# A hybrid two-layer decoder in split fp32: products with v of two groups moved behind a later group's scores, into one accumulator bank

## The chip, the core and the metric

The kernel runs on one core of a Trainium2 chip. The metric is the device time of one execution in microseconds (us). TensorE (PE) multiplies, VectorE (DVE) and ScalarE (ACT) work on tiles in SBUF and on PSUM, GpSimd (POOL) does a few small steps, and SyncE (SP) issues the DMAs that load weights.

## What is computed

Two layers on 256 positions of width 1024, 16 heads of 64, all in fp32:

```
h = x
for i in range(DEPTH):
    ln1_g, ln1_b, w1, w2, ln2_g, ln2_b = channel[i]
    h = layer_norm(DEEPNORM_ALPHA * h + mixers[i % N_MIXERS](h), ln1_g, ln1_b)
    h = layer_norm(DEEPNORM_ALPHA * h + squared_relu_mlp(h, w1, w2), ln2_g, ln2_b)
```

Layer 0 mixes by stick-breaking attention, where a weight is a sigmoid times a running product of others:

```
    log_keep = jnp.where(past, -jax.nn.softplus(z), 0.0)
    log_keep_between = lax.cumsum(log_keep, axis=3, reverse=True) - log_keep
    w = jnp.where(past, jnp.exp(jax.nn.log_sigmoid(z) + log_keep_between), 0.0)
    return jnp.einsum('bhqk,bhkd->bhqd', w.astype(v.dtype), v)
```

Layer 1 is block-sparse attention, which at 256 positions is one block: causal softmax attention with rotary positions. The MLP of both layers is `jnp.square(jax.nn.relu(x @ w1)) @ w2` with 4096 hidden values.

## The kernel before

Every fp32 operand of a projection is split into a high and a low part, and three products (high by high, high by low, low by high) make one. A weight comes in units of 1 MB: a DMA into one of three raw buffers (`Unit`, L249), two casts to `hi` on ScalarE and two subtractions to `lo` on VectorE (`split`, L205 and L206), into one of five split buffers. Activations stand transposed as `xh`, `xl`.

The heads of a layer go in four groups of four heads, each group in two pairs. The units of a layer's projections come in the order of `SEQ`: A0 to A3 give q and k of a group, V0 and V1 give v of two groups. Per group the chain is: projection (`qkT` in layer 0, `qk` and the transposes `tp` in layer 1), split of q and k (`qkh`, `qkl`), scores `sc` (`scores`, L438), weights (`weights`, L453), their transposes `pt_ps` (L501), a copy `pt` on ScalarE (L512), the products with v `o` (`mix`, L519) and their split `oh`, `ol`. In layer 0 the weights of a pair are two sigmoids on ScalarE (`keep`, `p`, L462), a scan on VectorE (L466), a mask on GpSimd (L470) and a product on VectorE (L473). In layer 1 they are maxima on VectorE (L479), four exponentials on ScalarE (L490) and a division by the sums (L497). Behind the groups come the output projection (`wo`, L614), LayerNorm (`norm`, L351) and the MLP (`up`, `down`).

PSUM has four accumulator banks (`acc`, one bank each: projections) and two double banks (`wk`, two banks each). The scores of a group take both `wk`, one per pair; each transposition of weights takes one, and so do the products with v of a group. A `wk` with scores comes free when ScalarE has read it for the last time.

The order of the instructions is fixed when the program is built. `Plan` (L64) keeps a clock per engine. An operation is given with an engine, a cost, a rank, what it follows (`after`) and which buffers it takes and gives. Projections are written straight into TensorE's order; the operations of a plan go into an engine's order where its clock lets them start, lowest rank first among those that could start within 0.25 us (`best`, L100). The costs are only used for that; on the chip the engines wait for each other by semaphores, each in its own fixed order. The scores are an operation of 1.55 (layer 0) or 1.8 (layer 1), rank 1, that takes both `wk` (L449); the products with v one of 1.36, rank 0.5, that takes one `wk` (L530).

Of the kernel before, what the change touches and what calls it, by code (L numbers as in the profile page):

```python
# [8 lines left out]
F32R = mybir.dt.float32r  # L9
# [5 lines left out]
P = 128  # L15
D = 1024
T = 256
NT = T // P
KT = D // P
HD = 64  # L20
# [11 lines left out]
MARGIN, WINDOW = 0.5, 0.25  # L32
X_LOADS = {0: 1, 1: 1, 2: 2, 4: 2, 6: 2}
WARM = 8

C_ID = 0
C_COS = C_ID + P
# [117 lines left out]
def trunk(ctx: ExitStack, tc: tile.TileContext, x, xt, cst, cstb, w, ln, out):  # L155
    nc = tc.nc
# [21 lines left out]
    def wbank(name):  # L178
        return wk.tile([P, 2, 512], F32, tag="wk", name=name)
# [231 lines left out]
    for l in range(DEPTH):  # L411
# [6 lines left out]
        def attend(g, pr, src, ready, give):  # L418

            box = {}

            def part(s):
                def go():
                    if s not in box:
                        box[s] = buf("qk" + "hl"[s], F32R)[:, :2 * T]  # L430
                    return box[s]
                return go
            qk = split(2 * T, part(0), part(1), src, after=ready, rank=0.9, take=[("t2k", 2, 2)], give=give)
            both[g].append((box, qk))
            if pr == 0:
                return

            def scores():  # L438
                for y, _ in both[g]:
                    sc = y["sc"] = wbank("sc")  # L440
                    for c0, nk, q0 in ((0, T, T - P), (T, P, 0)):
                        for i, (a, b) in enumerate(((0, 0), (0, 1), (1, 0))):
                            for j in range(2):
                                r = slice(j * HD, (j + 1) * HD)
                                mm(sc[:, j, c0:c0 + nk], y[a][r, q0:q0 + P], y[b][r, T:T + nk], c0 == 0 and i == 0, l == 0 and q0 == 0 and i == 2)
                for y, _ in both[g] if l else ():
                    for j in range(2):
                        mm(y["sc"][:, j, P:3 * P], identb, maskb, False, True)
            s = plan.op("pe", 1.8 if l else 1.55, scores, after=[y for _, y in both[g]], rank=1, take=[("wk", 2)], give=[("t2k", 4)])  # L449
            for q in range(2):  # L450
                weights(g, q, both[g][q][0], s)

        def weights(g, pr, box, s):  # L453
            sc = lambda: box["sc"][:, :, 0:3 * P]
            three = lambda y: y[:, :6 * P].rearrange("p (j e) -> p j e", j=2)
            if l == 0:
                def sig(name, scale):
                    def go():
                        y = box[name] = t3k.tile([P, 772], F32, tag="t3k", name=name)
                        if name == "keep":  # L460
                            nc.gpsimd.memset(y[:, 6 * P:6 * P + 1], 1.0)
                        nc.scalar.activation(three(y), sc(), AF.Sigmoid, scale=scale)  # L462
                    return go
                k = act(6 * P, sig("keep", -SCALE), after=[s], rank=0.7, take=[("t3k", 2)])
                b = act(6 * P, sig("p", SCALE), after=[k], rank=0.69, give=[("wk", 1)])
                c = dve(12 * P, lambda: nc.vector.tensor_tensor_scan(  # L466
                    box["keep"][:, 0:6 * P][:, ::-1], box["keep"][:, 0:6 * P][:, ::-1], ind[:, ::-1], 1.0,
                    op0=ALU.mult, op1=ALU.max), after=[k], rank=0.7)
                late = lambda: three(box["p"])[:, :, P:].rearrange("p j (a e) -> p j a e", e=P)
                z = plan.op("pool", 0.9, lambda: nc.gpsimd.affine_select(  # L470
                    out=late(), in_=late(), pattern=[[0, 2], [0, 2], [-1, P]], compare_op=ALU.is_gt, fill=0.0, base=0,
                    channel_multiplier=1), after=[b], rank=0.69)
                p = dve(6 * P, lambda: nc.vector.tensor_tensor(  # L473
                    box["p"][:, :6 * P], box["p"][:, :6 * P], box["keep"][:, 1:6 * P + 1], op=ALU.mult),
                    after=[z, c], rank=0.69, give=[("t3k", 1)])
            else:
                sm = smalla.tile([P, 16], F32, tag="sma", name="sma")
                part_of = [(0, T), (T, 3 * P)]
                mx = [dve(2 * (b - a), lambda t=t, a=a, b=b: nc.vector.tensor_reduce(  # L479
                    sm[:, 2 * t:2 * t + 2], box["sc"][:, :, a:b], axis=AX.X, op=ALU.max), after=[s], rank=0.7)  # L480
                    for t, (a, b) in enumerate(part_of)]
                ng = dve(10, lambda: nc.vector.tensor_scalar(sm[:, 4:8], sm[:, 0:4], -SCALE, None, op0=ALU.mult), after=mx, rank=0.7)
                ex = []
                for t, (a, b) in enumerate(part_of):
                    for j in range(2):
                        def go(t=t, j=j, a=a, b=b):
                            if t == 0 and j == 0:
                                box["p"] = t3k.tile([P, 772], F32, tag="t3k", name="p")
                            i = 2 * t + j
                            nc.scalar.activation(three(box["p"])[:, j, a:b], box["sc"][:, j, a:b], AF.Exp, scale=SCALE,  # L490
                                                 bias=sm[:, 4 + i:5 + i], accum_out=sm[:, 8 + i:9 + i])
                        ex.append(act(b - a + 290, go, after=[ng] + ex, rank=0.7, take=() if ex else [("t3k", 1)],
                                      give=[("wk", 1)] if t == 1 and j == 1 else ()))
                rc = dve(10, lambda: nc.vector.reciprocal(sm[:, 12:16], sm[:, 8:12]), after=ex, rank=0.65)
                for t, (a, b) in enumerate(part_of):
                    for j in range(2):
                        p = dve((b - a) * 0.54 + 55, lambda t=t, j=j, a=a, b=b: nc.vector.tensor_scalar(  # L497
                            three(box["p"])[:, j, a:b], three(box["p"])[:, j, a:b], sm[:, 12 + 2 * t + j:13 + 2 * t + j], None, op0=ALU.mult),
                            after=[rc], rank=0.65)

            def turn():  # L501
                ps = box["pp"] = wbank("pt_ps")
                for j in range(2):
                    pj = three(box["p"])[:, j, :]
                    nc.tensor.transpose(ps[:, j, 0:P], pj[:, T:T + P], ident)
                    nc.tensor.transpose(ps[:, j, P:T], pj[:, 0:P], ident)
                    nc.tensor.transpose(ps[:, j, T:T + P], pj[:, P:T], ident)
            tp = plan.op("pe", 0.66, turn, after=[p], rank=0.6, take=[("wk", 1)], give=[("t3k", 1)])

            def evac():  # L510
                box["pt"] = pts.tile([P, 2, 384], F32, tag="pt", name="pt")
                nc.scalar.copy(box["pt"], box["pp"][:, :, :384])  # L512
            ev = act(6 * P, evac, after=[tp], rank=0.6, take=[("pt", 1)], give=[("wk", 1)])

            pv[g].append((box, ev))
            if pr == 0:
                return

            def mix():  # L519
                if g // 2 not in OT:  # L520
                    OT[g // 2] = (st.tile([P, 4, T], F32R, tag="sh", name="oh"), st.tile([P, 4, T], F32R, tag="sl", name="ol"))
                o = pv[g][0][0]["o"] = wbank("o")
                for q in range(2):
                    for kt in range(2):
                        for j in range(2):
                            hd = 4 * g + 2 * q + j
                            pt = pv[g][q][0]["pt"][:, j, :]
                            nc.tensor.matmul(o[HD * j:HD * j + HD, q, kt * P:T], v[kt][:, hd * HD:(hd + 1) * HD],  # L528
                                             pt[:, 0:T] if kt == 0 else pt[:, T:T + P], start=kt == 0, stop=kt == 1)
            m = plan.op("pe", 1.36, mix, after=[e for _, e in pv[g]] + [vtok[g // 2]], rank=0.5,  # L530
                        take=[("wk", 1)] + ([("st", 1)] if g % 2 == 0 else []), give=[("pt", 2)])
            ps = slice(2 * (g % 2), 2 * (g % 2) + 2)
            mixed[g, 0] = mixed[g, 1] = split(2 * T, lambda: OT[g // 2][0][:, ps, :], lambda: OT[g // 2][1][:, ps, :],
                                              lambda: pv[g][0][0]["o"][:, :, :T], after=[m], rank=0.8, give=[("wk", 1)])

        def qkT(g, us):
            plan.wait(take=[("acc", 2)])
# [297 lines left out]
```

## Time and profile before

| | us |
|---|---|
| median of 3 runs (lowest, highest) | 595.88 (595.02, 596.15) |
| the profiled execution | 596.54 |
| its span, first to last instruction | 594.5 |
| busy: TensorE, VectorE, ScalarE, GpSimd | 584.9, 391.4, 288.4, 32.7 |
| mean granted TensorE clock | 0.996 |

The profile is of one execution; the span is what the trace covers of it. A TensorE that is busy is not at its peak, since matmuls overlap; what counts is the time from the start of one to the start of the next. In a row of the timeline the first number is the start in us from the span's start, the second the time that it took, and brackets at the end tell how long the engine had been idle and what ended that. On VectorE and ScalarE an instruction can start some 0.1 us before the one ahead of it has ended.

### The profile page before, as it was taken

What the parts mean: (1) busy time and instruction counts of PE and PEld (TensorE: products, weight loads), DVE (VectorE), ACT (ScalarE), POOL (GpSimd) and SP (SyncE); (2) the same over time, 40 slices, a digit from 0 to 9 for tenths busy, and PEclk for the clock granted to TensorE, in tenths of its full rate; (3) what the DMA queues carried; (4) which work ended last, traced back from release to release, by engine and by line L of the source; (5) the groups of instructions that cost most, each with busy time, mean ns of one, the idle gap of its engine ahead of it and who ended that gap; (6) DMA issues with size and microseconds to landing.
All of it is one profiled execution on the core that took longest, in us unless ns stands there. A gap on an engine that the chain in (4) does not pass through costs nothing.

```text
span 594.5 us, 8745 instructions
## 1 busy us (share of the span) xinstructions
PE 584.9 (98%) x3636; PEld 507.5 (85%) x3636; DVE 391.4 (66%) x485; ACT 288.4 (49%) x411; POOL 32.7 (5%) x38
## 2 busy tenths in 40 slices
PE   8999999999999999999999999999999999999995
PEld 6899987889899899898888788778898898899884
DVE  5779784878446555555789777768667437447445
ACT  5756574436444543543535754826446435435410
POOL 0102110000000000000032021000000000000000
PEclk9999999999999999999999999999999999999998
DMA  8977333175546346437175523443674364355101
GB/s 290 388 291 281 142 142 142 71 256 194 211 190 252 146 170 268 156 144 282 66 228 210 203 80 136 142 142 119 236 283 160 149 258 180 151 236 207 78 0 71
DMA packets 17895, 109.25 MB, mean 184 GB/s; under 512 B 1984, under 2 KB 2624, under 8 KB 5824
## 3 DMA queue, kind: packets, MB, share of 16 engines
q1 hardware_dynamic: 17856, 108.70, 49.2%
q8 instruction: 28, 0.46, 0.3%
q14 instruction: 11, 0.09, 0.0%
HBM read 107.64 MB, written 1.05 MB: 183 GB/s over the span
## 4 chain that ended last, share of the span: by engine, by line
PE 89%; DMA 4%; DVE 4%; ACT 1%; issue 1%; SPq 0%; POOL 0%; DVEq 0%; ACTq 0%
PE up_ps L191 29%; PE dn_ps L191 29%; PE wo_ps L191 8%; PE qk_ps L191 7%; PE v_ps L191 6%; DMA raw<-in_wqkv 3%; PE qkT_ps L191 2%; PE sc L191 2%; DVE lo L206 2%; PE o L528 2%; DMA raw<-in_first 1%; PE xt L386 1%; DVE keep L466 1%; ACT hi L205 1%; PE tp L574 1%
## 5 line engine op out<-in xcount | busy, mean ns | idle before, releaser
L206 DVE TENSOR_TENSOR lo<-raw,hi 128x1024 fp32r<-128x1024 f32 (+1 forms) x196 | 228.3, 1207 | 57.0 <-ACT hi L205 55.1
L205 ACT CAST hi<-raw 128x1024 fp32r<-128x1024 f32 (+1 forms) x196 | 191.8, 1032 | 70.5 <-issue 42.4
L191 PE MATMUL up_ps<-xh,hi 128*128 128x256 f32 x384 | 106.4, 277 | 0.0
L191 PE MATMUL up_ps<-xl,hi 128*128 128x256 f32 x384 | 106.1, 276 | 0.0
L191 PE MATMUL up_ps<-xh,lo 128*128 128x256 f32 x384 | 106.1, 276 | 0.0
L191 PE MATMUL dn_ps<-hi,hl 128*128 128x512 f32 x252 | 99.3, 394 | 0.0
L191 PE MATMUL dn_ps<-lo,hh 128*128 128x512 f32 x252 | 98.8, 392 | 0.0
L191 PE MATMUL dn_ps<-hi,hh 128*128 128x512 f32 x252 | 98.0, 389 | 0.0
L648 DVE SCALAR_TENSOR_TENSOR r<-up_ps,r 128x512 f32<-128x512 f32 x32 | 22.0, 687 | 77.9 <-ACT r L646 77.9
L191 PEld LDWEIGHTS up_ps<-xl,hi 128*128 128x128 f32 x384 | 72.1, 188 | 0.5
L191 PEld LDWEIGHTS up_ps<-xh,hi 128*128 128x128 f32 x384 | 72.1, 188 | 0.5
L191 PEld LDWEIGHTS up_ps<-xh,lo 128*128 128x128 f32 x384 | 72.1, 188 | 0.0
L646 ACT ACTIVATE r<-up_ps 128x512 f32<-128x512 f32 x32 | 19.1, 596 | 95.3 <-PE up_ps L191 95.3
L191 PEld LDWEIGHTS dn_ps<-lo,hh 128*128 128x128 f32 x252 | 47.3, 188 | 10.4
L191 PEld LDWEIGHTS dn_ps<-hi,hh 128*128 128x128 f32 x252 | 47.3, 188 | 10.0
L191 PEld LDWEIGHTS dn_ps<-hi,hl 128*128 128x128 f32 x252 | 47.4, 188 | 9.4
L191 PE MATMUL qkT_ps<-xh,hi 128*128 128x256 f32 x128 | 36.9, 289 | 0.0
L191 PE MATMUL qkT_ps<-xh,lo 128*128 128x256 f32 x128 | 36.2, 283 | 0.3 <-DVE lo L206 0.2
L191 PE MATMUL qkT_ps<-xl,hi 128*128 128x256 f32 x128 | 35.9, 280 | 0.0
L366 POOL TENSOR_TENSOR sm<-sm,one 128x1 f32<-128x1 f32 x8 | 7.9, 987 | 425.2 <-DVE sm L365 425.2
L205 ACT CAST xh<-xt 128x512 fp32r<-128x512 f32 x12 | 7.0, 586 | 41.1 <-PE xt L386 41.1
L191 PE MATMUL qk_ps<-hi,xh 128*128 128x512 f32 x64 | 26.3, 411 | 0.0
(106 smaller groups left out, 919.8 us busy)
## 6 DMA issues: line engine op xcount, KB each, us to landing
raw<-in_w SPq DMA_DIRECT2D x64, 1024.0 KB, 4.9
raw<-in_wqkv SPq DMA_DIRECT2D x22, 1024.0 KB, 5.1
raw<-in_wo SPq DMA_DIRECT2D x8, 1024.0 KB, 5.1
raw<-in_first SPq DMA_DIRECT2D x8, 256.0 KB, 5.9
gb<-in_l_ln_g SPq DMA_DIRECT2D x4, 512.0 KB, 3.9
gb<-in_l_ln_b SPq DMA_DIRECT2D x4, 512.0 KB, 5.1
h<-in_x SPq DMA_DIRECT2D x2, 512.0 KB, 7.3
h<-in_xt SPq DMA_DIRECT2D x3, 256.0 KB, 6.1
```

Of the source, the lines that this page charges most:

```text
L191: nc.tensor.matmul(ps, sta, mov, start=start, stop=stop)
L205: f = lambda: nc.scalar.copy(hi(), src())
L206: g = lambda: nc.vector.tensor_tensor(lo(), src(), hi().bitcast(F32), op=ALU.subtract)
L366: pw = plan.op("pool", 1.0, lambda: nc.gpsimd.tensor_tensor(rs, ve, nhalf, op=ALU.pow), after=[ep], rank=0)
L386: nc.tensor.transpose(XB[t, n][:, k * P:(k + 1) * P], h[t][:, (4 * n + k) * P:(4 * n + k + 1) * P], ident)
L466: c = dve(12 * P, lambda: nc.vector.tensor_tensor_scan(box["keep"][:, 0:6 * P][:, ::-1], box["keep"][:, 0:6 * P][:, ::-1], ind[:, ::-1], 1 ...
L528: nc.tensor.matmul(o[HD * j:HD * j + HD, q, kt * P:T], v[kt][:, hd * HD:(hd + 1) * HD], pt[:, 0:T] if kt == 0 else pt[:, T:T + P], start=k ...
L574: nc.tensor.transpose(tb[pr][:, c0:c0 + P], QK[g, t]["qk"][:, e * T + pr * P:e * T + pr * P + P], ident)
L646: nc.scalar.activation(box["r", n], ps, AF.Relu)
L648: return dve(512, lambda: nc.vector.scalar_tensor_tensor(box["r", n], ps, 0.0, box["r", n], op0=ALU.max, op1=ALU.mult), after=[a], rank=0. ...
```

## The change

Groups 0 and 1 of a layer lose their own operation for the products with v. In layer 0 the products of group 0 are issued in the operation of group 1's scores, right behind them, and those of group 1 behind group 2's; in layer 1 those of group 0 behind group 2's scores and those of group 1 behind group 3's (`MIX`). The joint operation costs 1.3 more, waits also for the transposed weights of the old group, and takes one `acc` bank besides the two `wk`. These products write one accumulator bank in place of a half-used double bank; groups 2 and 3 stay as they were. The mask on GpSimd is entered with 1.25 for 0.9.

```diff
+MIX = ({1: 0, 2: 1}, {2: 0, 3: 1})
...
-            s = plan.op("pe", 1.8 if l else 1.55, scores, after=[y for _, y in both[g]], rank=1, take=[("wk", 2)], give=[("t2k", 4)])
+            old = MIX[l].get(g)
+            if old is None:
+                s = plan.op("pe", 1.8 if l else 1.55, scores, after=[y for _, y in both[g]], rank=1, take=[("wk", 2)], give=[("t2k", 4)])
+            else:
+                s = plan.op("pe", 3.1 if l else 2.85, lambda: (scores(), mix(old)), after=[y for _, y in both[g]] + [e for _, e in pv[old]] + [vtok[old // 2]],
+                            rank=1, take=[("wk", 2), ("acc", 1)] + ([("st", 1)] if old % 2 == 0 else []), give=[("t2k", 4), ("pt", 2)])
+                mixed_from(old, s, ("acc", 1))
...
-                z = plan.op("pool", 0.9, lambda: nc.gpsimd.affine_select(
+                z = plan.op("pool", 1.25, lambda: nc.gpsimd.affine_select(
...
-            m = plan.op("pe", 1.36, mix, after=[e for _, e in pv[g]] + [vtok[g // 2]], rank=0.5,
-                        take=[("wk", 1)] + ([("st", 1)] if g % 2 == 0 else []), give=[("pt", 2)])
+            if g not in MIX[l].values():
+                bank = "wk" if g > 1 else "acc"
+                m = plan.op("pe", 1.36, lambda: mix(g), after=[e for _, e in pv[g]] + [vtok[g // 2]], rank=0.5,
+                            take=[(bank, 1)] + ([("st", 1)] if g % 2 == 0 else []), give=[("pt", 2)])
+                mixed_from(g, m, (bank, 1))
+
+        def mix(g):
...
+            o = wbank("o")[:, 0, :] if g > 1 else abank("o")
+            o = pv[g][0][0]["o"] = o.rearrange("p (q t) -> p q t", q=2)
...
+        def mixed_from(g, m, give):
...
-                                              lambda: pv[g][0][0]["o"][:, :, :T], after=[m], rank=0.8, give=[("wk", 1)])
+                                              lambda: pv[g][0][0]["o"], after=[m], rank=0.8, give=[give])
```

The planner then sets every engine's order anew, which the diff doesn't show. Three places follow. A line number of the change stands 2 to 15 above that of the same statement before.

VectorE in layer 0, around group 1's weights (lo8 to lo10 are splits of weight units, qkl those of group 1's q and k, keep the scans, p the products of L473, ol the split of group 0's products with v). Before:

```order
L206 TENSOR_TENSOR lo6_436<-raw6_371,hi6_435 128x1024 x2
L206 TENSOR_TENSOR ol_442<-o_443,oh_441 128x512
L206 TENSOR_TENSOR lo7_486<-raw7_452,hi7_485 128x1024 x2
L206 TENSOR_TENSOR lo8_518<-raw8_473,hi8_517 128x1024 x2
L206 TENSOR_TENSOR qkl_563<-qkT_ps_421,qkh_561 128x512
L206 TENSOR_TENSOR qkl_581<-qkT_ps_422,qkh_570 128x512
L206 TENSOR_TENSOR lo9_579<-raw9_508,hi9_578 128x1024 x2
L206 TENSOR_TENSOR lo10_626<-raw10_544,hi10_625 128x1024 x2
L466 SCALAR_TENSOR_TENSOR keep_640<-keep_640,const_112 128x768
L473 TENSOR_TENSOR p_653<-p_653,keep_640 128x768
L466 SCALAR_TENSOR_TENSOR keep_663<-keep_663,const_112 128x768
L473 TENSOR_TENSOR p_674<-p_674,keep_663 128x768
```

With the change:

```order
L208 TENSOR_TENSOR lo7_485<-raw7_444,hi7_484 128x1024 x2
L208 TENSOR_TENSOR lo8_517<-raw8_473,hi8_516 128x1024 x2
L208 TENSOR_TENSOR qkl_560<-qkT_ps_421,qkh_548 128x512
L208 TENSOR_TENSOR qkl_571<-qkT_ps_422,qkh_555 128x512
L208 TENSOR_TENSOR lo9_566<-raw9_504,hi9_565 128x1024 x2
L208 TENSOR_TENSOR lo10_628<-raw10_543,hi10_627 128x1024 x2
L474 SCALAR_TENSOR_TENSOR keep_636<-keep_636,const_112 128x768
L474 SCALAR_TENSOR_TENSOR keep_659<-keep_659,const_112 128x768
L481 TENSOR_TENSOR p_647<-p_647,keep_636 128x768
L481 TENSOR_TENSOR p_669<-p_669,keep_659 128x768
L208 TENSOR_TENSOR ol_616<-o_617,oh_615 128x512
```

The ol of group 0 went from ahead of lo7 to behind both products, and the second scan now stands ahead of the first product.

ScalarE in layer 1, around group 3's exponentials (p from sc; hi62 and hi63 are casts of wo's units, v1 the copy of v, oh the casts of the products with v). Before:

```order
L205 CAST hi62_3551<-raw62_3342 128x1024 x2
L490 ACTIVATE p_3569,sma_3420<-sc_3521,sma_3420 128x256 x2
L490 ACTIVATE p_3569,sma_3420<-sc_3521,sma_3420 128x128 x2
L490 ACTIVATE p_3588,sma_3421<-sc_3534,sma_3421 128x256
L601 COPY v1_96<-v_ps_3512 128x512
L205 CAST hi63_3593<-raw63_3407 128x1024 x2
L490 ACTIVATE p_3588,sma_3421<-sc_3534,sma_3421 128x256
L490 ACTIVATE p_3588,sma_3421<-sc_3534,sma_3421 128x128 x2
L205 CAST oh_3605<-o_3607 128x512
```

With the change:

```order
L207 CAST hi62_3518<-raw62_3315 128x1024 x2
L207 CAST oh_3384<-o_3563 128x512
L616 COPY v1_96<-v_ps_3473 128x512
L207 CAST hi63_3584<-raw63_3346 128x1024 x2
L498 ACTIVATE p_3590,sma_3405<-sc_3533,sma_3405 128x256 x2
L498 ACTIVATE p_3590,sma_3405<-sc_3533,sma_3405 128x128 x2
L498 ACTIVATE p_3598,sma_3406<-sc_3546,sma_3406 128x256 x2
L498 ACTIVATE p_3598,sma_3406<-sc_3546,sma_3406 128x128 x2
L207 CAST oh_3611<-o_3613 128x512
```

Group 1's oh, the copy of v and the two casts of hi63 now stand ahead of all eight exponentials.

TensorE in layer 1, from group 3's scores to group 2's products with v. Before, eighteen products of v stand between the masks and wo; the last three of them and what follows:

```order
L191 MATMUL v_ps<-hi_3268,xh 128x512
L191 MATMUL v_ps<-lo_3269,xh 128x512
L191 MATMUL v_ps<-hi_3268,xl 128x512
L191 MATMUL wo_ps<-hi_3306,oh 128x512
L191 MATMUL wo_ps<-lo_3307,oh 128x512
L191 MATMUL wo_ps<-hi_3306,ol 128x512
L528 MATMUL o<-pt,v_95 64x256 x2
L528 MATMUL o<-pt,v_96 64x128 x2
```

With the change, from the last mask on:

```order
L193 MATMUL sc<-masks 128x256
L543 MATMUL o<-pt,v_95 64x256 x2
L543 MATMUL o<-pt,v_96 64x128 x2
L543 MATMUL o<-pt,v_95 64x256 x2
L543 MATMUL o<-pt,v_96 64x128 x2
L193 MATMUL v_ps<-hi_3248,xh 128x512
L193 MATMUL v_ps<-lo_3249,xh 128x512
L193 MATMUL v_ps<-hi_3248,xl 128x512
L193 MATMUL wo_ps<-hi_3284,oh 128x512
L193 MATMUL wo_ps<-lo_3285,oh 128x512
L193 MATMUL wo_ps<-hi_3284,ol 128x512
L543 MATMUL o<-pt,v_95 64x256 x2
```

Group 1's products with v follow the masks, fifteen of the eighteen products of v have gone ahead of the scores, and group 2's products with v come after three of v and three of wo.

## Rows read from the trace of the kernel before

**Rows 1.** The page, busy time of each engine.
```profile
PE 584.9 (98%) x3636; PEld 507.5 (85%) x3636; DVE 391.4 (66%) x485; ACT 288.4 (49%) x411; POOL 32.7 (5%) x38
```

**Rows 2.** Waits of TensorE: for whom, us in total, times, longest.
```profile
PE pt_ps L505 <- DVE p L473: 0.5, 1, 0.5
```

**Rows 3.** Layer 0's MLP: stretch, length, busy us (count) by engine, granted clock, DMA.
```profile
131.00:290.00 159.00, 159.00 (x996) 142.42 (x995) 89.92 (x96) 71.28 (x87) 0.99 (x1) 1.00 0.51 194
```

**Rows 4.** TensorE's timeline, layer 0, group 0's products with v.
```profile
33.93 0.28 PE L191 MATMUL qkT_ps<-xh,lo 128*128 128x256 f32 x1
34.13 1.52 PE L528 MATMUL o<-pt,v 128*64 128x256 f32 x16
35.59 0.39 PE L191 MATMUL qkT_ps<-xh,hi 128*128 128x256 f32 x1
35.81 0.28 PE L191 MATMUL qkT_ps<-xl,hi 128*128 128x256 f32 x1
```

**Rows 5.** TensorE's timeline, layer 0, group 1's scores and what follows.
```profile
48.15 0.38 PE L191 MATMUL sc<-qkh 64*128 64x256 f32 x2
48.37 0.28 PE L191 MATMUL sc<-qkl,qkh 64*128 64x256 f32 x2
...
49.67 0.39 PE L191 MATMUL qkT_ps<-xh,hi 128*128 128x256 f32 x1
```

**Rows 6.** ScalarE's and VectorE's timeline, layer 0, group 1's weights.
```profile
43.88 2.00 ACT L205 CAST hi<-raw 128x1024 fp32r<-128x1024 f32 x2 [1.84 <-DMA raw<-in_wqkv]
...
47.24 1.28 DVE L206 TENSOR_TENSOR qkl<-qkT_ps,qkh 128x512 fp32r<-128x512 f32 x2
...
52.98 2.19 DVE L466 TENSOR_TENSOR_SCAN keep<-keep,const 128x768 f32<-128x768 f32 x1
55.27 1.14 DVE L473 TENSOR_TENSOR p<-p,keep 128x768 f32<-128x768 f32 x1
56.33 1.74 DVE L466 TENSOR_TENSOR_SCAN keep<-keep,const 128x768 f32<-128x768 f32 x1
58.18 0.96 DVE L473 TENSOR_TENSOR p<-p,keep 128x768 f32<-128x768 f32 x1
```

**Rows 7.** TensorE's timeline, layer 0, first transpose of group 1's weights.
```profile
56.55 0.30 PE L505 MATMUL pt_ps<-const,p 128*128 128x128 f32 x1 [0.48 <-DVE p L473]
```

**Rows 8.** TensorE's timeline, layer 1, around group 2's products with v.
```profile
381.15 0.39 PE L191 MATMUL v_ps<-hi,xl 128*128 128x512 f32 x1
...
382.17 1.52 PE L528 MATMUL o<-pt,v 128*64 128x256 f32 x16
383.62 0.51 PE L191 MATMUL wo_ps<-hi,oh 128*128 128x512 f32 x1
...
384.20 0.39 PE L191 MATMUL wo_ps<-hi,ol 128*128 128x512 f32 x1
384.43 0.39 PE L191 MATMUL wo_ps<-hi,oh 128*128 128x512 f32 x1
```

**Rows 9.** ScalarE's timeline, layer 1, exponentials of group 3, first and fourth sum.
```profile
378.55 0.47 ACT L490 ACTIVATE p<-sc,sma 128x256 f32<-128x256 f32 x1 [1.07 <-DVE sma L482]
...
380.06 0.21 ACT L490 ACTIVATION_READ_ACCUMULATOR p<-sc,sma 128x1 f32 x1
...
381.58 0.59 ACT L601 COPY v<-v_ps 128x512 f32<-128x512 f32 x1 [0.86 <-PE v_ps L191]
382.06 2.00 ACT L205 CAST hi<-raw 128x1024 fp32r<-128x1024 f32 x2
```

**Rows 10.** TensorE's first products, then stretches behind the last matmul (columns as above).
```profile
1.38 3.60 PE L285 MATMUL warm_ps<-masks 128*128 128x512 bf16 x8 [1.38 <-POOL keep L461]
...
6.26 0.28 PE L191 MATMUL qkT_ps<-xh,lo 128*128 128x256 f32 x1
...
587.10:589.80 2.70, 0.00 (x0) 0.00 (x0) 2.56 (x7) 0.00 (x0) 0.99 (x1) 1.00 0.00 0
589.80:594.50 4.70, 0.00 (x0) 0.00 (x0) 1.45 (x3) 0.00 (x0) 0.00 (x0) 0.51 0.31 112
```

More of the change, by code (lines that the diff above doesn't have):

```diff
@@ L517, in weights @@
                 return
[L519 to L529, printed above, removed]
@@ new lines, in mix @@
+        def mix(g):
+            if g // 2 not in OT:
+                OT[g // 2] = (st.tile([P, 4, T], F32R, tag="sh", name="oh"), st.tile([P, 4, T], F32R, tag="sl", name="ol"))
+            o = wbank("o")[:, 0, :] if g > 1 else abank("o")
+            o = pv[g][0][0]["o"] = o.rearrange("p (q t) -> p q t", q=2)
+            for q in range(2):
+                for kt in range(2):
+                    for j in range(2):
+                        hd = 4 * g + 2 * q + j
+                        pt = pv[g][q][0]["pt"][:, j, :]
+                        nc.tensor.matmul(o[HD * j:HD * j + HD, q, kt * P:T], v[kt][:, hd * HD:(hd + 1) * HD],
+                                         pt[:, 0:T] if kt == 0 else pt[:, T:T + P], start=kt == 0, stop=kt == 1)
```

## Prediction

> **What bounds the kernel now.** I read the page's busy times first: TensorE is busy for 584.9 of 594.5 us [rows 1]. The list of TensorE's waits comes next. After the first microseconds its one entry of note is 0.5 us, a transpose of group 1's weights in layer 0 that waits for VectorE's product at L473 [rows 2]. The table by stretch shows the same for the MLP: TensorE busy for all of 159 us, VectorE for 90 and ScalarE for 71 [rows 3]. So the order of TensorE's work is nearly free of holes, and the end is set by its sum. Two things can change the time: what it loses when it switches between kinds of matmul, and holes that the new order opens. A hole in the attention of either layer is not paid back later, since the MLP behind it runs without any slack on TensorE.
>
> **What a switch costs.** Products of 256 columns start every 0.12 us. The last one before group 0's products with v starts 0.20 us ahead of them, and the first one behind them holds the engine for 0.22 us [rows 4]. So entering costs 0.08, and the first full product after leaving 0.10. The sixteen parts themselves take 1.46 us. The scores take 1.52 from their start to the next projection [rows 5].
>
> In layer 0 the change takes away one entry and one leaving per pair (scores, products with v) and adds one passage from scores to products that no row shows. Bounds of a pair's gain: nothing, if that passage costs as much as both, and 0.36, if it is free (0.08 + 0.10, and as much again for the last parts, which run out before the next kind starts). I take 0.2, near the middle, since the nearest row, the plain passage [rows 4], costs half of that sum; no row shows a passage dearer than an entry and a leaving together, so I leave out a loss. In layer 1 the scores end with mask products over the whole array, so only a passage of the plain kind goes: 0 to 0.2 a pair, taken as 0.1. Two pairs in each layer: **-0.6 us**, between 0 and -1.1. The Trainium skill, in TensorEngine Tiling (Array Packing), Key Properties, says that changing the tiling mode drains the engine; scores are tiles of 64 rows and products tiles of 64 columns, so by it the passage is not free, and -0.6 would shrink to about -0.3.
>
> **Layer 0, group 1's scores.** Without the products of group 0 ahead of them these scores come earlier: 48.15 [rows 5], less 35.59 - 33.93 = 1.66, plus 0.12 for the plain step, less 0.10 for the slow first product [rows 4], plus 0.35 for three products that now stand ahead of them: 46.86. Their third part needs qkl. VectorE makes it from 47.24 on (1.28 for the two, so the first ends at about 47.9) [rows 6], and it can't be earlier: it stands behind two lo of weight unit 8, which wait for two casts that ScalarE began at 43.88, when that unit's load had landed [rows 6]. The change leaves that order as it was but for one ol fewer. The third part was due 0.22 after the start [rows 5], at 47.08, and can run at 48.0: a new wait of **0.9 us**. It lies between 0, should the load land a microsecond earlier, and 1.0. Behind it TensorE has nothing it could do out of order.
>
> **Layer 0, group 1's transposes.** The scores end at 48.0 - 0.22 + 1.52 = 49.3. Products with v follow until 50.7, then 57 projection products of 0.12 with their first slow one: TensorE reaches the transposes at 57.4. They need the first product of L473. Before, VectorE ran scan, product, scan, product: 52.98 for 2.19, 55.27 for 1.14, 56.33 for 1.74, 58.18 for 0.96 [rows 6]. The start of the first scan stays, since four lo stand ahead of it whose loads don't move. Now both scans come first. The second one ends at 55.1 + 1.74 to 2.19 (the two lengths that rows 6 show), the product takes 0.96 to 1.14 behind it, and the transposes follow 0.14 later, as now (55.27 + 1.14 to 56.55 [rows 6, 7]): 58.0 to 58.6. I take 58.35, so a wait of **0.95 us**, bounds 0.6 to 1.2, in the place of the present one of 0.5 [rows 2, 7], **-0.5**. These two waits are tied: if the first is short, TensorE stands the longer at the second, for it is VectorE that sets 58.35. The second product ends 0.9 after the first, and TensorE comes to its transposes 0.95 after it came to the others, so nothing is added there.
>
> The ol of group 0 now comes behind both products on VectorE, at about 59 to 59.7, and until then its accumulator bank is held. Two more banks are next asked for by group 3's projection, some 2 us after that; this costs nothing while that cover stands. The pool operation's new number (1.25 for 0.9) is a due time in the planner and adds no work. Loads keep their sequence on SP.
>
> **Layer 1, group 2's products: the largest term.** Let S be the end of group 3's scores on TensorE. There TensorE used to have eighteen products of v and three of wo in hand before group 2's products with v. Now there are group 1's products with v (1.45), three of v (383.62 to 384.43, as those of wo behind products with v do now: 0.81) and three of wo with the passage (381.15 to 382.17 less one product: 0.79) [rows 8]. TensorE comes to group 2's products at S + 3.05.
>
> These still take a double bank, and both double banks hold group 3's scores until ScalarE has done the exponentials. On ScalarE four things now stand ahead of the first exponential: the cast oh of group 1, the copy of v, and two casts of the last wo unit. The copy can begin 0.43 after the last v product starts (381.15 to 381.58 [rows 8, 9]), and that start is S + 1.45 + 0.58 (383.62 to 384.20), so at S + 2.46; oh is through by then. The copy takes 0.48 (381.58 to 382.06), two casts 2.0, and the first four exponentials with their sums 1.72 (378.55 to 380.06 + 0.21) [rows 9]. The first double bank comes free at S + 6.66. The wait is 6.66 - 3.05 = **3.6 us**; I take 3.5, as the two casts overlap what follows by 0.1, and bounds of 3.2 and 3.8. Behind the waiting products stand the transposes of group 3 and the rest of wo, with nothing else that TensorE could do. VectorE's maxima for that bank, which the exponentials need, stand no later in its order than before and don't decide. Behind the hole all inputs are early, so no further wait follows.
>
> **The clock.** After the last matmul, which ended at 587.1, the granted clock stayed at 1.00 up to 589.8 and was 0.51 after it [rows 10]. So it fell within 2.7 us of idling. TensorE will idle for some 3.4 us in the hole of layer 1 (3.5 less what the last wo product still runs). The nearest row thus says that the clock falls to 1.2 GHz in the hole or just behind it. The price: nothing, if it holds; at most 2.4 us, as at the start, where the eight warm-up products of 512 columns took 0.45 each, twice the usual 0.23 (384.20 to 384.43 [rows 8]), and full speed came at 6.2, 4.8 us after the first of them at 1.38 [rows 10], half of which is lost. I take **1.4 us**, a little above the middle, since by the row the fall comes shortly before work resumes. The Trainium skill, in TensorE: Matmul & The Clock Gate (HAM oscillation), says that a long wait between matmuls throttles the engine again and the next work starts cold; by it the sum keeps this term, without it it would be 1.4 less.
>
> **Sum.** -0.6 + 0.9 + 0.95 - 0.5 + 3.5 + 1.4 = +5.65. The profiled execution took 596.54, 0.66 above the median of the runs, 595.88. On its own time the sum gives 602.2, on the median **601.5 us**. A change within 0.2%, 1.2 us, can't be told from none.
>
> **The rivals.**
> 1. *The clock holds.* Nothing in the trace of before has a hole as long as this in mid-program, so only the end speaks for a fall, and there TensorE never resumes. Time 595.88 + 4.25 = 600.1. By the Trainium skill's rule above this would not happen. Chance 0.36.
> 2. *The lost time is given back, and it comes out not slower.* Place: the MLP. If weights (load, cast, lo) paced TensorE there, the hole of layer 1 would let units run ahead and be recovered. It decides once TensorE shows waits in the MLP. Against it: busy for 159 of 159 us there [rows 3], and only five split units fit. Time 595.88 - 0.6 = 595.3. Chance 0.06.
> 3. *The loads of layer 0 land earlier than in this one execution,* so that both waits there shrink to 0.6 together, and the clock holds: 595.88 - 0.6 - 0.5 + 0.6 + 3.5 = 598.9. Chance 0.05.
> 4. *The change doesn't do what it says:* products of a group could stand apart from the scores. The order of the instructions shows them together at all four places, so I give this no chance of its own.
>
> **How the numbers follow.** Forecast 0.50, the three rivals 0.36, 0.06 and 0.05; 0.03 is left for more than 603.4, should the clock stay low for longer than at the start. The bounds of layer 0's two waits together (0.6 to 2.2), of layer 1's (3.2 to 3.8), of the switches (0 to -1.1) and of the clock (0 to 2.4), with the -0.5, reach from 598.1 to 603.8; I cut this to 599.2 to 603.0, which leaves out rivals 2 and 3 and the ends. Faster by over 0.2%: 0.04, most of rival 2; within 0.2%: 0.04; slower: 0.92.
>
> **What would show it.** Right: a wait of 3 to 4 us by o on ScalarE's p at L498 in layer 1; a wait of near 1 us by sc on qkl and one of near 1 us by pt_ps on L481 in layer 0; a stretch of some 3 us behind the long wait with a granted clock near 0.5 and products of 512 columns at 0.43. Wrong: no such wait of o, or the wait and an unchanged time, or a clock of 1.00 throughout with 600.

## The result, and the profile after

The changed kernel took **599.57 us** (median of 4 runs, 598.70 to 599.96), the kernel before 596.01 (595.02 to 596.16) on the same chip: ratio 1.0062, 95% interval 1.0050 to 1.0074, so it is slower. In a later comparison with more runs of the kernel before it took 600.12 against 595.45, ratio 1.0072 (1.0060 to 1.0085).

| | before | after |
|---|---|---|
| profiled execution, us | 596.54 | 599.2 |
| its span | 594.5 | 597.2 |
| mean granted TensorE clock | 0.996 | 0.995 |

The busy line of the page after, which answers to [rows 1]:

```profile
PE 583.6 (98%) x3636; PEld 507.0 (85%) x3636; DVE 393.5 (66%) x485; ACT 288.3 (48%) x411; POOL 34.4 (6%) x38
```

TensorE has the same number of instructions and is busy for 1.3 us less, in a span that is 2.7 longer. The list of TensorE's waits after, which answers to [rows 2], says where the difference stands (columns: line, tile waited for, us in total, times, longest):

```profile
PE o L543 <- ACT p L498: 3.5, 1, 3.5
PE warm_ps L287 <- POOL keep L469: 1.4, 1, 1.4
PE qkT_ps L193 <- DVE lo L208: 0.7, 3, 0.2
PE qkT_ps L193 <- ACT hi L207: 0.6, 1, 0.6
```

One long wait, the forecast one: group 2's products with v wait for ScalarE's exponentials, 3.5 us. Two forecast waits of layer 0 are not there, neither `sc` on `qkl` nor `pt_ps` on the product of L481. TensorE's timeline of layer 1 after, from group 1's products with v on, answers to [rows 8]:

```profile
376.98 1.52 PE L543 MATMUL o<-pt,v 128*64 128x256 f32 x16
378.43 0.51 PE L193 MATMUL v_ps<-hi,xh 128*128 128x512 f32 x1
...
379.71 0.40 PE L193 MATMUL wo_ps<-hi,ol 128*128 128x512 f32 x1
383.59 2.83 PE L543 MATMUL o<-pt,v 128*64 128x256 f32 x16 [3.48 <-ACT p L498]
386.35 0.51 PE L193 MATMUL wo_ps<-hi,oh 128*128 128x512 f32 x1
```

ScalarE's timeline over the same stretch answers to [rows 9]:

```profile
378.55 0.59 ACT L207 CAST oh<-o 128x512 fp32r<-128x512 f32 x1 [3.77 <-PE o L543]
379.44 0.59 ACT L616 COPY v<-v_ps 128x512 f32<-128x512 f32 x1 [0.31 <-PE v_ps L193]
379.93 1.99 ACT L207 CAST hi<-raw 128x1024 fp32r<-128x1024 f32 x2
381.82 0.48 ACT L498 ACTIVATE p<-sc,sma 128x256 f32<-128x256 f32 x1
...
383.32 0.22 ACT L498 ACTIVATION_READ_ACCUMULATOR p<-sc,sma 128x1 f32 x1
```

The scores of group 3 end at 376.98 (S in the prediction). ScalarE has been idle for 3.77 us when the joint products have ended; it casts `oh`, copies v, makes two casts, and begins the exponentials at 381.82. The fourth sum ends at 383.54 and TensorE goes on at 383.59. The forecast had the double bank free at S + 6.66, which is 383.64.

The 16 parts of that `o` take 2.76 us to the next product, where group 1's took 1.45. The windows around them (columns as in [rows 3]) show what changed for them:

```profile
380.00:382.90 2.90, 0.11 (x1) 0.00 (x0) 1.89 (x2) 2.90 (x8) 0.00 (x0) 1.00 0.15 62
383.10:386.30 3.20, 2.71 (x16) 1.68 (x16) 3.06 (x13) 2.10 (x11) 0.00 (x0) 0.50 0.61 179
386.60:390.00 3.40, 3.40 (x20) 2.80 (x20) 2.08 (x3) 3.15 (x4) 0.00 (x0) 1.00 0.24 101
```

The granted clock, before DMA share and GB/s at the end of each row, is still 1.00 (2.4 GHz) up to 382.90. It is 0.50 (1.2 GHz) from 383.10 on, so it fell in the hole, some 0.6 us before TensorE resumed; it stays there to the end of these products and is 1.00 again behind them. By the Trainium skill, TensorE: Matmul & The Clock Gate (HAM oscillation), a long wait between matmuls throttles the engine; this trace agrees.

The MLP of layer 0 is as full as in [rows 3], so nothing is paid back there:

```profile
131.00:290.00 159.00, 159.00 (x995) 142.34 (x994) 91.79 (x98) 73.08 (x90) 0.98 (x1) 1.00 0.49 188
```

The MLP of layer 1, which stands behind the hole, takes 178.2 us in both traces (first `up` product to the end of the last matmul), so nothing is paid back there either.

### The profile page after: what moved, and what is told of

Read it like the earlier page. It is cut to its first block, busy times and chain, and to the rows that moved or that the text cites. A ratio compares the mean times of both kernels' runs of the same rounds, so it can differ in the third digit from the quotient of the medians.

```text
span 597.2 us, 8746 instructions
## 1 busy us (share of the span) xinstructions
PE 583.6 (98%) x3636; PEld 507.0 (85%) x3636; DVE 393.5 (66%) x485; ACT 288.3 (48%) x411; POOL 34.4 (6%) x38
## 4 chain that ended last, share of the span: by engine, by line
PE 96%; DMA 1%; ACT 1%; DVE 1%; SPq 0%; issue 0%; DVEq 0%
PE up_ps L193 29%; PE dn_ps L193 29%; PE v_ps L193 7%; PE qk_ps L193 7%; PE wo_ps L193 7%; PE qkT_ps L193 7%; PE sc L193 2%; PE o L543 2%; DMA raw<-in_first 1%; PE xt L388 1%; PE pt_ps L514 1%; PE ht_ps L696 1%; PE pt_ps L515 1%; PE tp L589 1%; PE pt_ps L513 1%; PE dn_end L193 0%
## 5 line engine op out<-in xcount | busy, mean ns | idle before, releaser
L207 ACT CAST hi<-raw 128x1024 fp32r<-128x1024 f32 (+1 forms) x196 | 191.8, 1032 | 71.7 <-issue 42.4
L193 PE MATMUL qkT_ps<-xh,hi 128*128 128x256 f32 x128 | 36.2, 283 | 0.7 <-ACT hi L207 0.6
L193 PE MATMUL wo_ps<-hi,oh 128*128 128x512 f32 x64 | 26.2, 409 | 0.0
```

Of the source, the lines that this page charges most:

```text
L193: nc.tensor.matmul(ps, sta, mov, start=start, stop=stop)
L207: f = lambda: nc.scalar.copy(hi(), src())
```

## The experiments

Times are medians; the ratio is to the kernel before on the same chip (595.57 us for the first four, 595.45 for the next four, 595.73 for the last).

| kernel | us | ratio (95% interval) |
|---|---|---|
| layer 0 alone | 595.07 | 0.9990 (0.9981 to 0.9999) |
| layer 1 alone | 600.61 | 1.0081 (1.0068 to 1.0095) |
| hole filled | 598.33 | 1.0042 (1.0028 to 1.0056) |
| two casts on GpSimd | 596.31 | 1.0015 (1.0006 to 1.0024) |
| the change again | 600.12 | 1.0072 (1.0060 to 1.0085) |
| credit in layer 1 | 594.83 | 0.9989 (0.9980 to 0.9998) |
| credit in both | 595.29 | 0.9998 (0.9986 to 1.0010) |
| credit, group 3 alone | 594.92 | 0.9995 (0.9987 to 1.0004) |
| bank alone | 596.64 | 1.0021 (1.0012 to 1.0030) |

**Layer 0 alone.**

```diff
-MIX = ({1: 0, 2: 1}, {2: 0, 3: 1})
+MIX = ({1: 0, 2: 1}, {})
...
-                bank = "wk" if g > 1 else "acc"
+                bank = "wk" if g > 1 or l else "acc"
...
-            o = wbank("o")[:, 0, :] if g > 1 else abank("o")
+            o = wbank("o")[:, 0, :] if g > 1 or l else abank("o")
```

> Layer 0 has the changed order and banks, layer 1 those of the kernel before. Theory A (layer 0's new order is better by itself: switches saved, the 0.5 us wait of the transposes gone, no new wait): the traces of the two kernels, laid side by side at equal products, differ by 1.7 to 2.1 us at the end of layer 0's attention, so 596.0 - 1.9 = 594.1 us. Theory B (the new order is as forecast, and the changed kernel's one execution had lucky loads): -0.4 of switches + 0.9 + 0.95 - 0.5, so about 597 us, with waits of sc on qkl and of pt_ps on the product of L481. Theory C (it gains only the switches, the rest differs from execution to execution): 595.4 to 595.7.

0.5 us under the kernel before: theory B, the forecast's, falls, and theory A, read from two traces laid side by side, promised too much. Between A and C the time points to C. Yet its profile has one of the forecast waits, larger than forecast (TensorE's timeline, then ScalarE's ahead of it):

```profile
56.32 0.30 PE L513 MATMUL pt_ps<-const,p 128*128 128x128 f32 x1 [1.31 <-DVE p L481]
```

```profile
47.78 2.00 ACT L207 CAST hi<-raw 128x1024 fp32r<-128x1024 f32 x2 [2.31 <-DMA raw<-in_wqkv]
49.68 0.81 ACT L470 ACTIVATE keep<-sc 128x768 f32<-128x768 f32 x1
```

The sigmoids of group 1 stand behind the casts of unit 10 (V1's first), which waited for their load until 47.78, and the scans behind its two `lo`. In the profile of the kernel with casts on GpSimd, whose layer 0 is the same, that cast began at 46.01 and the transposes waited for nothing:

```profile
46.01 2.00 ACT L207 CAST hi<-raw 128x1024 fp32r<-128x1024 f32 x2 [0.33 <-DMA raw<-in_wqkv]
```

So this wait comes and goes with the landing of one load, taken against TensorE's own progress.

**Layer 1 alone.**

```diff
-MIX = ({1: 0, 2: 1}, {2: 0, 3: 1})
+MIX = ({}, {2: 0, 3: 1})
...
-                z = plan.op("pool", 1.25, lambda: nc.gpsimd.affine_select(
+                z = plan.op("pool", 0.9, lambda: nc.gpsimd.affine_select(
...
-                bank = "wk" if g > 1 else "acc"
+                bank = "wk" if g > 1 or not l else "acc"
...
-            o = wbank("o")[:, 0, :] if g > 1 else abank("o")
+            o = wbank("o")[:, 0, :] if g > 1 or not l else abank("o")
```

> Layer 1 has the changed order and banks, layer 0 those of the kernel before. Theory A: the hole of 3.5 us in front of group 2's products, plus 1.3 for a clock that falls, less 0.2 of switches: 596.0 + 4.6 = 600.6 us, and together with layer 0 alone the two differences add up to that of the whole change (+3.6). Theory B (layer 0 costs time on the whole): layer 1 alone then is worth less than 3.6, under 599.6 us. Where the clock holds: 599.3.

600.61, that is 5.0 over the kernel before: theory A. The wait is 3.5 again, and the clock falls again. With layer 0 alone, the halves add up to +4.5; the change again stands at +4.7.

**The hole filled.**

```diff
-                m = plan.op("pe", 1.36, lambda: mix(g), after=[e for _, e in pv[g]] + [vtok[g // 2]], rank=0.5,
+                m = plan.op("pe", 1.36, lambda: ([nc.tensor.matmul(banks[1][1], identb, warm, start=True, stop=True) for _ in range(14 if l and g == 2 else 0)], mix(g)), after=[e for _, e in pv[g]] + [vtok[g // 2]], rank=0.5,
```

> The changed kernel with 14 idle products of 512 columns (0.23 us each, 3.2 us in all) put on TensorE right in front of group 2's products of layer 1, into a bank that is not in use yet; nothing else moves. If group 2's products took 2.76 us instead of 1.45 because the clock fell in the hole, they take 1.45 again, the granted clock is 1.00 through the stretch and the time is 599.6 - 1.3 = 598.3 us, the mean granted clock 0.998 or more. If they are slow for another reason, a start after a wait for ScalarE, 2.76 stays and so does 599.6. Should the idle products end later than the wait, they cost up to 0.3.

598.33, as expected. TensorE's timeline of this kernel, then the window over it:

```profile
380.56 3.20 PE L529 MATMUL wo_ps<-masks 128*128 128x512 bf16 x14
384.21 1.52 PE L543 MATMUL o<-pt,v 128*64 128x256 f32 x16 [0.45 <-ACT p L498]
385.66 0.50 PE L193 MATMUL wo_ps<-hi,oh 128*128 128x512 f32 x1
```

```profile
380.00:386.00 6.00, 5.55 (x35) 2.82 (x34) 4.28 (x10) 5.94 (x20) 0.00 (x0) 1.00 0.31 100
```

The exponentials are no earlier, the `o` begins where it did after its scores, and 14 products of no use make the kernel faster: the clock stays at 1.00 and the 16 parts take 1.45. The clock's price, by the medians, is 599.57 or 600.12 less 598.33: 1.2 to 1.8 us. The rows give it without what layer 0 does: from layer 1's first projection product to the first of its MLP (TensorE's timeline, first of the changed kernel, then of this one) it takes 118.48 against 117.16 us, so 1.3. With layer 1 alone and with the change again the stretch takes 118.80 and 118.73, so 1.6.

```profile
293.20 0.39 PE L193 MATMUL qk_ps<-hi,xh 128*128 128x512 f32 x1
...
411.68 0.39 PE L193 MATMUL up_ps<-hi,xh 128*128 128x512 f32 x1
```

```profile
293.81 0.39 PE L193 MATMUL qk_ps<-hi,xh 128*128 128x512 f32 x1
...
410.97 0.39 PE L193 MATMUL up_ps<-hi,xh 128*128 128x512 f32 x1
```

**Two casts on GpSimd.**

```diff
-    def split(n, hi, lo, src, after, rank=1, take=(), give=(), scale=None):
+    def split(n, hi, lo, src, after, rank=1, take=(), give=(), scale=None, other=False):
...
-        f = lambda: nc.scalar.copy(hi(), src())
+        f = lambda: (nc.gpsimd.tensor_copy if other else nc.scalar.copy)(hi(), src())
...
-                              lambda c0=c0, c1=c1: self.raw[:, c0:c1, :], after=[ld] + [k.first for k in self.tok[:1]],
+                              lambda c0=c0, c1=c1: self.raw[:, c0:c1, :], other=i == 63, after=[ld] + [k.first for k in self.tok[:1]],
```

> The changed kernel; the two casts to hi of the last wo unit of layer 1 run on GpSimd instead of ScalarE, and no order of TensorE, VectorE or SyncE moves. Theory A (the exponentials that free the double bank stand behind these casts, 1.0 us each): the wait of group 2's products shrinks from 3.5 to 1.5 us, the clock holds over so short a hole, and the time is 599.6 - 2.0 - 1.3 = 596.3 us (597.6 if the clock falls all the same). Rival (VectorE's maxima, or the copies ahead, set the exponentials): the wait stays above 3 us and the time near 599.6. If GpSimd makes the casts so late that wo waits for them, a new wait stands in front of the last wo products: up to 3 us of the gain lost.

596.31, as theory A says; its runs lie between 595.62 and 597.52, so that the last digit agrees is luck. The order of TensorE, VectorE and SyncE is that of the changed kernel; GpSimd makes the two casts in 3.02 us, well ahead of need. ScalarE's timeline, then TensorE's:

```profile
379.15 0.59 ACT L616 COPY v<-v_ps 128x512 f32<-128x512 f32 x1 [0.31 <-PE v_ps L193]
379.63 0.48 ACT L498 ACTIVATE p<-sc,sma 128x256 f32<-128x256 f32 x1
```

```profile
381.41 1.52 PE L543 MATMUL o<-pt,v 128*64 128x256 f32 x16 [1.60 <-ACT p L498]
```

The exponentials follow the copy of v at once, the wait is 1.60, and over this shorter hole the clock holds (the parts take 1.45). The two casts that stood ahead on ScalarE were the cause of 1.9 of the 3.5 us; VectorE's maxima, in an unchanged order, allowed the exponentials 1.9 us earlier.

**The change again**, unaltered.

> The changed kernel unaltered, on the chip of the next three. If the two halves add up (-0.5 for layer 0 alone, +5.0 for layer 1 alone), it stands 4.5 us above the kernel before; if layer 0's order helps or harms what follows in layer 1, the difference stays at the 3.6 of its first comparison. Its layer 0 shows which of its waits come back: where the load of the second unit of group 3's projection lands at 47.5 us or later, a wait of the first transposes of group 1 by 0.5 to 1.3 us; where it lands before 46.8, none. The one wait that must be there each time is that of group 2's products in layer 1, 3.5 us.

600.12 and +4.7: the halves add up. The 3.5 are there, the transposes' wait is not. (The load that this expectation means is unit 10, V1's first, not one of group 3's projection.) Its casts began at 47.45, between the two bounds of the text; TensorE had lost 0.6 earlier in this execution, waiting for a `lo` of V0, and so came to the transposes later. The clock fell elsewhere than in the first profile:

```profile
381.20:385.60 4.40, 0.91 (x11) 0.66 (x12) 3.36 (x6) 4.40 (x16) 0.00 (x0) 1.00 0.17 48
385.80:389.00 3.20, 3.20 (x18) 2.41 (x14) 3.10 (x10) 2.13 (x6) 0.00 (x0) 0.53 0.74 307
```

It is 1.00 through the whole hole and falls when TensorE is back at work (`o` began at 384.8, the fall is at 386.0).

**Credit in layer 1.** The planner reckons the weights of a joint piece from 1.3 us ahead of the piece's end, about where its scores end.

```diff
-                weights(g, q, both[g][q][0], s)
+                weights(g, q, both[g][q][0], Early(s, 1.3) if l and old is not None else s)
...
+class Early:
+    def __init__(self, tok, by):
+        self.tok, self.by = tok, by
+
+    def at(self, eng):
+        t = self.tok.at(eng)
+        return None if t is None else t - self.by
```

> The changed kernel, in which the planner is told that the scores of a joint piece of layer 1 are done 1.3 us ahead of the piece's end, so that the exponentials go into ScalarE's order ahead of the copy of v and the casts; TensorE's order in layer 1 then moves too. Theory A (the hole is one of order on ScalarE alone, and the idea of the change is sound without it): no wait over 0.3 us in layer 1, clock 1.00, and the time is that of layer 0 alone less 0.2 for the switches of layer 1: 0.7 under the kernel before, 594.9 us. Rival (joint pieces in layer 1 cost time in themselves, since the exponentials always start 1.45 us after their scores end, or the double banks come free too late in any order): a wait of 1 us or more stays and the time is 596 us or above.

594.83: theory A, and no entry of layer 1 is left among TensorE's waits. ScalarE's timeline, then TensorE's:

```profile
376.15 0.48 ACT L498 ACTIVATE p<-sc,sma 128x256 f32<-128x256 f32 x1
...
377.65 0.22 ACT L498 ACTIVATION_READ_ACCUMULATOR p<-sc,sma 128x1 f32 x1
...
379.30 0.59 ACT L616 COPY v<-v_ps 128x512 f32<-128x512 f32 x1 [0.98 <-PE v_ps L193]
379.79 1.99 ACT L207 CAST hi<-raw 128x1024 fp32r<-128x1024 f32 x2
```

```profile
374.10 1.52 PE L543 MATMUL o<-pt,v 128*64 128x256 f32 x16
...
379.57 0.39 PE L193 MATMUL wo_ps<-hi,ol 128*128 128x512 f32 x1
379.88 1.52 PE L543 MATMUL o<-pt,v 128*64 128x256 f32 x16
```

The double bank is free at 377.9, ahead of the copy and the casts, and `o` begins without a wait. TensorE's order has moved as well: fifteen products of v, not three, now stand between the joint piece and `o`. With three, TensorE would have come to it 3.05 after its scores' end at 374.10 (the forecast's sum), at 377.15 and 0.7 ahead of the bank, so this run doesn't show the earlier exponentials alone closing the hole. It has the lowest median here, 0.1% under the kernel before by an interval that barely leaves out no change; two other versions stand within 0.3 us of it. Of layer 1 the rows give more: from the first projection product to the first of the MLP (TensorE's timeline, first of this kernel, then of the one before) it takes 113.57 against 113.59 us.

```profile
293.08 0.39 PE L193 MATMUL qk_ps<-hi,xh 128*128 128x512 f32 x1
...
406.65 0.39 PE L193 MATMUL up_ps<-hi,xh 128*128 128x512 f32 x1
```

```profile
295.33 0.39 PE L191 MATMUL qk_ps<-hi,xh 128*128 128x512 f32 x1
...
408.92 0.39 PE L191 MATMUL up_ps<-hi,xh 128*128 128x512 f32 x1
```

Without the hole, then, layer 1 gains nothing from joint pieces; the gain of this version is layer 0's.

**Credit in both layers.** The argument is `s if old is None else Early(s, 1.3)`.

> As the one before, with the same credit of 1.3 us in layer 0 too, so that the sigmoids and scans of groups 1 and 2 of layer 0 go ahead of the weights' casts and lo. If the transposes' wait in layer 0 comes from scans that stand behind the lo of the last loaded unit, it goes below 0.5 us whatever the load does, and the time is 0.5 under that of the kernel with the credit in layer 1 alone: 594.4 us. If the casts and lo that now come later are themselves what TensorE needs next, a wait by qkT_ps on lo takes its place: 594.9 us or more.

595.29, no better than with the credit in layer 1 alone, and the wait of the transposes is larger:

```profile
PE pt_ps L513 <- DVE p L481: 1.7, 1, 1.7
```

```profile
48.53 1.05 ACT L207 CAST hi<-raw 128x1024 fp32r<-128x1024 f32 x1 [2.67 <-DMA raw<-in_wqkv]
49.49 0.81 ACT L470 ACTIVATE keep<-sc 128x768 f32<-128x768 f32 x1
```

The credit moved only one of unit 10's two casts behind the sigmoids. The other still stands ahead of them and here waited for its load until 48.53, while TensorE's transposes had moved forward. Neither expectation held: the wait follows the landing of the load, which this order leaves in front of the sigmoids.

**Credit for group 3 alone.** The argument is `Early(s, 0.5) if l and g == 3 else s`.

> The changed kernel with a credit of 0.5 us for group 3's scores of layer 1 alone. ScalarE's order up to the exponentials stays as it is in the changed kernel (oh, copy of v, two casts ahead of them); TensorE has fifteen more products of wo in front of group 2's products with v. Theory A (a hole has two cures: the releaser earlier, or more work in front): the exponentials end at the same time after the scores as in the changed kernel, the wait falls from 3.5 to 0.2 us, the clock stays at 1.00, and the time is 599.6 - 3.3 - 1.3 = 595.0 us. Rival (the work that is put in front is missing later, at the third wo unit or the last group's products): a wait of 1 us or more there, 596 us or above.

594.92, as theory A says. ScalarE's order up to the exponentials is that of the changed kernel, and 15 more products of `wo` cover the time that they need; no wait of layer 1 is left in the list. Its layer 1 still takes 114.27 us where that of the kernel with the credit in layer 1 takes 113.57 (first projection product to first of the MLP), so this order costs 0.7 that the list of waits doesn't show. Work in front is thus enough to close the hole; an earlier releaser on its own took 1.9 of it with the casts on GpSimd, and with the credit in layer 1 both act together.

**The kernel before, twice more**, for its trace (595.15 and 595.66 us).

> The kernel before, unaltered, for its trace. Theory A (when a load of layer 0 lands is a matter of the execution): the load of the first unit of group 3's projection, which landed at 46.28 us in the execution that the forecast was read from and at 43.90 in the layer-0 order of the kernel with layer 1 alone, lands somewhere between 43.5 and 46.5, and the wait of 0.5 us by group 1's transposes need not come back. Theory B (it is a matter of the order): 46 us again, and the wait with it.

> The same once more, with the same two theories: a second, different landing speaks for A, 46 us in both for B.

Theory A. (The landings that the text names, 46.28 and 43.90, are those of unit 9, group 3's second; they are now 43.08, a little ahead of the range that the text gives, and 43.55.) Unit 8, on which the forecast rests, shows the same. Its casts in the first of the two:

```profile
40.67 2.00 ACT L205 CAST hi<-raw 128x1024 fp32r<-128x1024 f32 x2 [1.84 <-DMA raw<-in_wqkv]
```

They began at 43.88 in the execution that the forecast was read from [rows 6], and at 40.67 and 41.14 here. In neither is there a wait of the transposes.

**The bank alone.** `MIX = ({}, {})`, and the pool operation's old 0.9.

> Only the bank part of the change: products with v of groups 0 and 1 stay a piece of their own (no joint pieces, the pool operation's old number), but lie in one accumulator bank. In layer 0 TensorE's order up to group 1's scores is that of the kernel before, so group 0's products stand alone in front of 102 projection products of 256 columns, which take 281 ns and start every 0.1178 us in all four traces of that order, and 276 ns and 0.1133 us in the eight traces with joint pieces. Theory A (the slower step comes with a lone piece of products at that place): 281 ns again. Theory B (it comes with the double bank): 276 ns. For the time: if the bank alone brought layer 0's gain, 595.0 us; if the gain needs the joint pieces, 595.4 us or, as the double banks that come free early let the planner move pieces in layer 1 too, up to 1 us more.

596.64, 0.9 us slower: the bank alone is no gain, since the planner moves layer 1's pieces and a wait of 0.6 us by `pt_ps` on `ol` comes up there. For layer 0's step between products it is theory A. TensorE's groups by form from 36.2 to 45.2 us (count: shortest, median and longest ns, first and last start) of this kernel, of the one before and of the changed one:

```profile
L193 PE MATMUL qkT_ps<-xh,lo x27: 281/281/281, 36.0 to 45.2; 128*128 128x256 f32 x27
```

```profile
L191 PE MATMUL qkT_ps<-xh,lo x27: 281/281/281, 35.9 to 45.1; 128*128 128x256 f32 x27
```

```profile
L193 PE MATMUL qkT_ps<-xh,hi x28: 276/276/276, 36.0 to 45.2; 128*128 128x256 f32 x28
```

Three kinds take turns, so 27 in 9.2 us (26 steps of three) is one product every 0.118, and 28 in 9.2 one every 0.114; the traces' unrounded starts give 0.1178 and 0.1133. (The lone products of group 0 stand in front of 105 such products, not 102.) A lone piece doesn't always bring the slower step: in the kernel before, the 30 products behind group 1's lone products, from 63.3 us on, have a median of 276 ns.

## Why the prediction came out as it did

Its sign and its largest terms were right; the time, 601.5, was 1.9 above the first measurement and 1.4 above the second.

- **Layer 1, +3.5: right**, by its own steps. The hole measured 3.5 in three profiles; taking the two casts away took 1.9 from it, and moving the exponentials ahead, with twelve more products of v in front, took it all.
- **The clock, +1.4: right in size**, 1.3 to 1.6 by layer 1's rows. The step "the fall comes shortly before work resumes" held in one profile of three; in the other two it came behind the hole. Rival 1 (the clock holds) didn't happen in any of these profiles, but it seems to in executions without a trace: of the thirteen of the kernels with the 3.5 us hole (the changed kernel twice, layer 1 alone), three have a mean granted clock of 0.998, as high as any of the kernel before, and the other ten 0.990 to 0.995. The three took 598.70, 598.50 and 599.40 us, each the shortest of its kernel, by 0.5 to 1.2; a fall as in the profiles, 3.4 us at 0.50, would have lowered the mean by 0.003. So the term is a matter of the execution too.
- **The switches, -0.6: too large by half.** A pair of layer 0 saves what the step said, as TensorE's timeline after shows beside [rows 4, 5]:

```profile
45.77 0.28 PE L193 MATMUL qkT_ps<-xh,lo 128*128 128x256 f32 x1
45.97 0.39 PE L193 MATMUL sc<-qkh 64*128 64x256 f32 x2
...
47.50 1.52 PE L543 MATMUL o<-pt,v 128*64 128x256 f32 x16
48.95 0.39 PE L193 MATMUL qkT_ps<-xh,hi 128*128 128x256 f32 x1
49.17 0.28 PE L193 MATMUL qkT_ps<-xl,hi 128*128 128x256 f32 x1
```

  Scores 1.53 and products 1.45 take as long as alone; the entry (0.20 less 0.12) and the slow first product (0.22 less 0.12) are saved once, 0.18 a pair. In layer 1 the saving was put at 0.1 a pair and is nil (113.57 against 113.59). That makes -0.4, nearer the -0.3 that the prediction worked out by the Trainium skill, TensorEngine Tiling (Array Packing), Key Properties: the passage from scores to products is not free.
- **Layer 0's waits, +0.9 + 0.95 - 0.5: the step that failed.** "The change leaves that order as it was" is true, and the time still didn't stand, for the step took the landing of one execution for a property of the kernel. Unit 8's casts began at 43.88 in that execution alone; in all twelve other traces they began between 40.6 and 42.4, in either order. With that the first wait, of `sc` on `qkl`, is gone from each of the eight traces with joint pieces in layer 0, and the present 0.5 that was to be saved is an exception too: it stands in one of four traces of the old order. The second wait is real where unit 10 lands late against TensorE's own progress: 1.3 and 0.5 in two of the seven traces in the order of the change, none in the list of the others. Layer 0 was put at +0.95 with its switches (taken at -0.4) and measured -0.5 (-1.1 to -0.1 by the interval).
- Rival 3, earlier loads, was thus half right: it had the cause, but bound it to a clock that holds, and gave it 0.05.
- **What the sum left out:** the slower step of the projection behind group 0's lone products. Some 103 steps of 0.1178 and not 0.1133 are 0.46 us, which the joint pieces win in layer 0.

## What to carry to other kernels

Where a planner sets the order, joining two operations hides the end of the first half: all that follows from it is planned from the end of the whole, and here ScalarE put four other things in front of the exponentials that free a bank. Give the planner the inner end, which here also put more work in front of the piece that waits, or put the work there; filling the hole with idle products gets back the clock alone. And before a wait on a load is entered in a sum, read its landing from more than one execution.

## What the runs showed of the hardware that was not expected

- Products of 256 columns ran in two steps, 0.1133 and 0.1178 us (276 and 281 ns each), and kept the one that they had begun with for a hundred products. Behind the lone products of group 0 it was 0.1178 in all five traces that have them there, with either bank; without that piece it was 0.1133 in all eight. Why is open.
- The granted clock fell to 0.50 once inside the hole, 0.6 us before TensorE resumed, and twice behind it, 0.7 and 1.2 us after TensorE had resumed, with holes of the same 3.5 us; in three executions without a trace its mean speaks against a fall there.
- One load of layer 0 landed up to 3 us apart in executions of the same kernel, which may well be the larger part of the 1.5 us that its times are spread over; that wasn't tested, nor whether the chip has a part in it.
